# SSD chunks of a hybrid encoder step: decay multiply and D term of the chunks taken off GpSimd

## The chip, the cores and the metric

The kernel runs on one core of one Trainium2 chip. The metric is the device time of one execution in microseconds, the median of several executions. The core's engines are named PE (TensorE, matrix products), DVE (VectorE), ACT (ScalarE), POOL (GpSimd) and SP (which issues DMAs). Each runs its own instructions in a fixed order and waits for the others by semaphores.

## The reference, cut to what matters

One layer of an encoder is run on 592 columns: 16 meta tokens, 512 prompt tokens, 64 sample tokens. Three branches share one input projection: a Mamba-2 SSD branch, an S5 branch with a gated linear unit (GLU), and stick-breaking attention. Each is lifted to 1024 channels, weighted by a sigmoid gate and summed; an output projection and an MLP follow. The change is in the SSD branch:

```python
    decay = jnp.exp(jnp.where(causal, seg, -jnp.inf))
    cb = jnp.einsum('bcign,bcjgn->bcijg', cm, bm)
    y_diag = jnp.einsum('bcijgh,bcjghp->bcighp', cb[..., None] * decay * dt[:, :, None], x)
    to_end = jnp.exp(a_cum[:, :, -1:] - a_cum) * dt
    blk_states = jnp.einsum('bcjgn,bcjgh,bcjghp->bcghpn', bm, to_end, x)
    ...
    y_off = jnp.einsum('bcign,bcghpn,bcigh->bcighp', cm, s_in, jnp.exp(a_cum))
    ...
    y = y[:, front:front + T] + d_skip.reshape(SSD_GROUPS, SSD_HPG)[:, :, None] * xs
    y = y.reshape(bsz, T, SSD_WIDTH) * jax.nn.silu(z)
```

There are 16 heads of 64 channels. `x` times `to_end` feeds the state of the next chunk; `d_skip` times `x`, one number per head, is added to the output.

## The kernel before

**Dense work.** Every projection is split into tiles of 288 output columns. Operands are split into a high and a low part, so each 128-deep step k is three matmuls (L336, L337, L338, in `mm3`). A tile of the GLU and of the attention lift has four steps (12 matmuls), the others eight (24). The result `ps_d` lies in one of three PSUM buffers (pool `psd`), and the next tile in that buffer waits until ACT or DVE has read it. The GLU runs for m in 0..7: two sigmoid tiles, which ACT reads (`gls`, L250) before DVE multiplies `gt` by it, then two product tiles, which DVE reads as `mix<-ps_d,gt`. The attention lift (`ocx`) follows, then the SSD lift `la`, which reads `yah` and `yal` for k = 0..7. Weights are split by ACT (`w_hi`, L253) and DVE (`w_lo`, L217).

**Side work.** The SSD branch is a generator, `ssd`, from which the dense loop pulls steps while GLU and lift run. It goes over six chunks: chunk 0 of 16 columns, chunks 1 to 4 of 128, chunk 5 of 64. For each chunk `turned` transposes on PE (`ps_bt`, `ps_x`), copies `bt` on ACT (L1240) and multiplies x by dt on DVE (`xd`). `late_x` multiplies `xd` by `tend` into `xe` (L1260). `decay` has ACT take Exp of half of `ar` into `a` twice (L1270), DVE subtract 16 times (L1272), ACT take Exp of `ar` (L1273). `weigh` multiplies `ar` by `cb` on DVE and sets `ya` to x times D (L1285). `outputs` multiplies on PE into `ps_y` (L1318), `state` into `ps_st` (L1293), and `gather` adds `ps_y` to `ya` on DVE. After the last chunk `ya` is gated, normed and split into `yah` (ACT, L257) and `yal` (DVE), which `la` reads.

**Order.** The instructions of all engines are put in order by a scheduler that simulates a timeline of the whole program; the source gives dependences, priorities (`urgent` for weights and for reading `ps_d`) and the order within a pulled step. An edit of one step can thus move instructions far from it. Sigmoid and Exp need different ACT tables, and going from one to the other is an `ACT_TABLE_LOAD`.

Of the kernel before, what the change touches and what calls it, by code (L numbers as in the profile page):

```python
# [11 lines left out]
AF = mybir.ActivationFunctionType  # L12
OP = mybir.AluOpType
# [163 lines left out]
def body(tc, io):  # L177
    nc = tc.nc
    V, S, G, PE, SP = nc.vector, nc.scalar, nc.gpsimd, nc.tensor, nc.sync
# [4 lines left out]
    with ExitStack() as ctx:  # L184
# [13 lines left out]
        A = lambda n, i=0, w=1: pa[:, PA[n][0] + i:PA[n][0] + i + w]  # L198
# [17 lines left out]
        def tt(e, o, a, b, op):  # L216
            e.tensor_tensor(o, a, b, op=op)  # L217
# [226 lines left out]
        with urgent():  # L444
            for ps, cols in zip(pss, halves):
                n = cols.stop - cols.start
# [757 lines left out]
        def ssd():  # L1204
            yp = late["y"] = tc.alloc_tile_pool(name="late_y", bufs=1)
            ya = late["ya"] = yp.tile([128, 8, T], F32, name="ya", tag="x2")
            dp = tc.alloc_tile_pool(name="ssd", bufs=1)
            d2 = tc.alloc_tile_pool(name="ssd2", bufs=2)
            dt, acm, tend, bd = (sv[n] for n in ("dt", "acm", "tend", "bd"))
# [46 lines left out]
            def late_x(c):  # L1256
                t0, n = chunks[c]
                e = env[c]
                e["xe"] = xe = dp.tile([128, 16, 64], F32, name="xe", tag="xe")
                tt(G, xe[:n], e["xd"][:n], tend[:n, c, :].unsqueeze(2).to_broadcast([n, 16, 64]), OP.mult)  # L1260

            def decay(c):

# [14 lines left out]
            def weigh(c):  # L1278
                t0, n = chunks[c]
                e = env[c]  # L1280
                ar, cb = e["ar"], e["cb"]
                for g in range(2):
                    tt(V, ar[:n, 8 * g:8 * g + 8, :n], ar[:n, 8 * g:8 * g + 8, :n],
                       cb[:n, g, :n].unsqueeze(1).to_broadcast([n, 8, n]), OP.mult)
                tt(G, ya[:, :, t0:t0 + n], e["xc"][:, 0:8, :n], A("d_ssd", 0, 8).unsqueeze(2).to_broadcast([128, 8, n]),  # L1285
                   OP.mult)

            def state(c, st):
                t0, n = chunks[c]
# [41 lines left out]
            yield  # L1331
            turned(0)
            late_x(0)
            yield
            st = state(0, None)
            turned(1)
            late_x(1)
            fetch_chunk(2)
            yield
# [25 lines left out]
            for c in range(1, 6):  # L1365
                if c < 5:
                    turned(c + 1)
                weigh(c)
                if c == 5:
                    normed(0, 0)  # L1370
# [19 lines left out]
                if c < 5:  # L1390
                    late_x(c + 1)
# [80 lines left out]
        for m2 in range(4):  # L1472
            w = None
            for j in range(2):
                m = 2 * m2 + j
# [186 lines left out]
```

## Time and profile before

| | |
|---|---|
| median of three runs | 1111.87 us (1111.23, 1111.87, 1114.11) |
| the profiled execution | 1113.19 us, span 1111.5 us, granted clock 0.998 |
| PE busy | 1095.5 us |
| DVE busy | 795.7 us |
| ACT busy | 540.7 us |
| POOL busy | 125.4 us |

The span is the profiled stretch of one execution; the 1.7 us to its time are start and end around it. Times are microseconds; a granted clock of 1.00 is TensorE's full 2.4 GHz. In a timeline a row is a run of like instructions: start, length, engine, line, operation, output and inputs, shape, count, and in brackets idle time before it with what released it. Matmuls are pipelined: one takes 0.29 us and the next starts 0.13 us after it.

### The profile page before, as it was taken

What the parts mean: (1) busy time and instruction counts of PE and PEld (TensorE: products, weight loads), DVE (VectorE), ACT (ScalarE), POOL (GpSimd) and SP (SyncE); (2) the same over time, 40 slices, a digit from 0 to 9 for tenths busy, and PEclk for the clock granted to TensorE, in tenths of its full rate; (3) what the DMA queues carried; (4) which work ended last, traced back from release to release, by engine and by line L of the source; (5) the groups of instructions that cost most, each with busy time, mean ns of one, the idle gap of its engine ahead of it and who ended that gap; (6) DMA issues with size and microseconds to landing.
All of it is one profiled execution on the core that took longest, in us unless ns stands there. A gap on an engine that the chain in (4) does not pass through costs nothing.

```text
span 1111.5 us, 21286 instructions
## 1 busy us (share of the span) xinstructions
PE 1095.5 (99%) x8532; PEld 1056.3 (95%) x8532; DVE 795.7 (72%) x1390; ACT 540.7 (49%) x928; POOL 125.4 (11%) x193
## 2 busy tenths in 40 slices
PE   9999999999999999999999999999999999999998
PEld 8998999999998999897888999999999999999998
DVE  7968579965767466468989754477867776786787
ACT  6465466633365545365657333354444444444443
POOL 1087233011000000021310001200000000000000
PEclk9999999999999999999999999999999999999999
DMA  7653223566754353187445533222232223123222
GB/s 274 149 138 114 94 80 132 136 190 171 222 178 151 112 169 136 64 267 247 133 139 178 173 109 115 99 76 77 76 114 80 74 84 123 60 77 133 77 82 80
DMA packets 80594, 144.04 MB, mean 130 GB/s; under 512 B 26512, under 2 KB 40688, under 8 KB 79984
## 3 DMA queue, kind: packets, MB, share of 16 engines
q1 hardware_dynamic: 80496, 142.69, 41.7%
q8 instruction: 67, 1.10, 0.4%
q14 instruction: 31, 0.25, 0.1%
HBM read 117.40 MB, written 24.38 MB: 128 GB/s over the span
## 4 chain that ended last, share of the span: by engine, by line
PE 83%; DVE 8%; ACT 3%; POOL 2%; issue 2%; DMA 2%; SPq 1%; POOLq 0%; ACTq 0%; DVEq 0%
PE ps_d L336 19%; PE ps_d L337 19%; PE ps_d L338 18%; PE ps_x L1581 3%; PE ps_x L1580 3%; PE ps_x L1582 3%; PE ps_o L895 2%; PE ps_z L895 2%; PE ps_y L1581 1%; PE ps_y L1580 1%; PE ps_y L1582 1%; PE ps_y L1318 1%; DVE w_lo L217 1%; DVE ya L217 1%; PE ps_z L1581 1%
## 5 line engine op out<-in xcount | busy, mean ns | idle before, releaser
L253 ACT ACTIVATE w_hi<-w_raw 128x1024 fp32r<-128x1024 f32 (+1 forms) x150 | 151.9, 1012 | 219.8 <-PE ps_d L337 142.2
L336 PE MATMUL ps_d<-hh,w_hi 128*128 128x288 f32 (+1 forms) x864 | 258.2, 299 | 0.0
L337 PE MATMUL ps_d<-hl,w_hi 128*128 128x288 f32 (+1 forms) x864 | 258.0, 299 | 0.0
L338 PE MATMUL ps_d<-hh,w_lo 128*128 128x288 f32 (+1 forms) x864 | 258.0, 299 | 0.0
L217 DVE TENSOR_TENSOR w_lo<-w_raw,w_hi 128x1024 fp32r<-128x1024 f32 (+1 forms) x150 | 180.3, 1202 | 95.2 <-ACT w_hi L253 91.9
L337 PEld LDWEIGHTS ps_d<-hl,w_hi 128*128 128x128 f32 x864 | 162.6, 188 | 0.9 <-issue 0.3
L338 PEld LDWEIGHTS ps_d<-hh,w_lo 128*128 128x128 f32 x864 | 162.6, 188 | 0.6
L336 PEld LDWEIGHTS ps_d<-hh,w_hi 128*128 128x128 f32 x864 | 162.7, 188 | 0.2
L336 PE MATMUL ps_d<-x2h,w_hi 128*128 128x288 f32 x512 | 151.2, 296 | 0.0
L337 PE MATMUL ps_d<-x2l,w_hi 128*128 128x288 f32 x512 | 151.1, 295 | 0.0
L338 PE MATMUL ps_d<-x2h,w_lo 128*128 128x288 f32 x512 | 150.3, 295 | 0.0
L336 PEld LDWEIGHTS ps_d<-x2h,w_hi 128*128 128x128 f32 x512 | 96.2, 188 | 0.1
L338 PEld LDWEIGHTS ps_d<-x2h,w_lo 128*128 128x128 f32 x512 | 96.2, 188 | 0.1
L337 PEld LDWEIGHTS ps_d<-x2l,w_hi 128*128 128x128 f32 x512 | 96.2, 188 | 0.0
L253 ACT ACTIVATE w_hi<-ws 128x1024 fp32r<-128x1024 f32 x32 | 34.0, 1061 | 55.0 <-PE ps_y L1581 21.6
L1581 PE MATMUL ps_x<-ftl,w_hi 128*128 128x288 f32 x192 | 56.7, 295 | 0.5 <-DVE ftl L217 0.5
L1580 PE MATMUL ps_x<-fth,w_hi 128*128 128x288 f32 x192 | 56.8, 296 | 0.2 <-ACT s L1600 0.2
L1582 PE MATMUL ps_x<-fth,w_lo 128*128 128x288 f32 x192 | 56.4, 294 | 0.0
L1531 ACT ACTIVATE fr<-ps_d 128x288 f32<-128x288 f32 x64 | 25.7, 402 | 55.8 <-PE ps_d L338 55.8
L217 DVE TENSOR_TENSOR w_lo<-ws,w_hi 128x1024 fp32r<-128x1024 f32 x32 | 39.1, 1220 | 12.6 <-ACT w_hi L253 12.6
L336 PE MATMUL ps_d<-ybx,w_hi 128*128 128x288 f32 x128 | 39.7, 310 | 3.0 <-DVE mix L217 2.3
L906 DVE TENSOR_TENSOR_SCAN aw<-col,aw 128x400 f32<-128x400 f32 (+4 forms) x36 | 30.7, 898 | 16.6 <-ACT aw L250 16.6
(471 smaller groups left out, 2643.3 us busy)
## 6 DMA issues: line engine op xcount, KB each, us to landing
w_raw<-wts SPq DMA_DIRECT2D x150, 512.0 KB, 3.5
g_scr<-go SPq DMA_DIRECT2D x24, 288.0 KB, 2.8
gt<-g_scr SPq DMA_DIRECT2D x24, 288.0 KB, 3.0
ar<-ac_scr SPq DMA_DIRECT2D x4, 1024.0 KB, 7.5
x_scr<-cs SPq DMA_DIRECT2D x10, 297.5 KB, 3.1
xc<-x_scr SPq DMA_DIRECT2D x4, 640.0 KB, 7.4
xt<-xT SPq DMA_DIRECT2D x8, 296.0 KB, 5.6
z_scr<-zs SPq DMA_DIRECT2D x8, 288.0 KB, 5.0
```

Source lines behind the costliest of these rows:

```text
L217: e.tensor_tensor(o, a, b, op=op)
L253: S.activation(hi, x, AF.Copy)
L336: PE.matmul(ps, wh[:, c], xh[:, k, cols], start=start and k == 0, stop=False)
L337: PE.matmul(ps, wh[:, c], xl[:, k, cols], start=False, stop=False)
L338: PE.matmul(ps, wl[:, c], xh[:, k, cols], start=False, stop=stop and k == kt - 1)
L895: mm = lambda *a, **b: PE.matmul(*a, skip_group_check=True, **b)
L906: V.tensor_tensor_scan(x, one.to_broadcast([128, n]), x, 1.0, op0=OP.mult, op1=OP.mult)
L1318: PE.matmul(py[oo, 128 * (h // 2):128 * (h // 2) + n], a, b, start=step == 0, stop=step == 1, skip_group_check=True)
L1531: S.activation(r[:, cols], ps, AF.Relu)
L1580: PE.matmul(ps, w[0][:, o], fh[:, k], start=first and k == 0, stop=False, skip_group_check=True)
L1581: PE.matmul(ps, w[0][:, o], fl[:, k], start=False, stop=False, skip_group_check=True)
L1582: PE.matmul(ps, w[1][:, o], fh[:, k], start=False, stop=k == 3, skip_group_check=True)
```

## The change

In `late_x` the product of `xd` and `tend`, six times in a run, goes from POOL to DVE. In `weigh` the product of x and D of a chunk, one POOL instruction for eight blocks of 128 channels, becomes eight ACT copies, one for each block, with D as a scale that differs by partition: 40 copies for chunks 1 to 5, of 128 columns (32) or 64 (8). POOL keeps two memsets there.

```diff
             def late_x(c):
...
-                tt(G, xe[:n], e["xd"][:n], tend[:n, c, :].unsqueeze(2).to_broadcast([n, 16, 64]), OP.mult)
+                tt(V, xe[:n], e["xd"][:n], tend[:n, c, :].unsqueeze(2).to_broadcast([n, 16, 64]), OP.mult)
...
             def weigh(c):
...
-                tt(G, ya[:, :, t0:t0 + n], e["xc"][:, 0:8, :n], A("d_ssd", 0, 8).unsqueeze(2).to_broadcast([128, 8, n]),
-                   OP.mult)
+                for m in range(8):
+                    S.activation(ya[:, m, t0:t0 + n], e["xc"][:, m, :n], AF.Copy, scale=A("d_ssd", m))
```

The scheduler puts all engines in another order. On ACT, from the `bt` of chunk 4 on, before:

```order
L1240 ACTIVATE bt<-ps_bt 128x128
L253 ACTIVATE w_hi<-w_raw 128x1024
L1270 ACTIVATE a_6029<-ar 64x1024 x2
L250 ACT_TABLE_LOAD
L250 ACTIVATE gls<-ps_d 128x288 x2
L253 ACTIVATE w_hi<-w_raw 128x1024
L250 ACTIVATE gls<-ps_d 128x288
L1273 ACT_TABLE_LOAD
L1273 ACTIVATE ar<-ar 128x2048
L1240 ACTIVATE bt<-ps_bt 64x128
L250 ACT_TABLE_LOAD
L250 ACTIVATE gls<-ps_d 128x288
```

and now, from the `bt` of the same chunk on (`ya<-xc,pa` are the new copies, of chunk 3 and, 64 wide, of chunk 5):

```order
L1240 ACTIVATE bt<-ps_bt 128x128
L1286 ACTIVATE ya<-xc,pa 128x128 x8
L250 ACT_TABLE_LOAD
L250 ACTIVATE gls<-ps_d 128x288
L1270 ACT_TABLE_LOAD
L1270 ACTIVATE a_6050<-ar 64x1024 x2
L253 ACTIVATE w_hi<-w_raw 128x1024
L1286 ACTIVATE ya<-xc,pa 128x64 x8
L250 ACT_TABLE_LOAD
L250 ACTIVATE gls<-ps_d 128x288
L1273 ACT_TABLE_LOAD
L1273 ACTIVATE ar<-ar 128x2048
```

The next two are a table load and the third sigmoid. Between the first sigmoid and the third stood nothing but one `w_hi`; now four table loads, both Exps and eight copies stand there, and eight copies ahead of the first. Over the whole program the table loads go from 33 to 34.

On DVE, a little ahead of that, from the end of chunk 2 into chunk 3, before:

```order
L217 TENSOR_TENSOR ya<-ps_y,ya 128x8x128
L217 TENSOR_TENSOR mix<-ps_d,gt 128x288
L217 TENSOR_TENSOR st<-st,ps_st 128x512
L217 TENSOR_TENSOR cb<-ps_bt,cst 128x128 x2
L217 TENSOR_TENSOR mix<-ps_d,gt 128x288
L217 TENSOR_TENSOR w_lo<-w_raw,w_hi 128x1024
L1272 TENSOR_SCALAR ar<-ar,acm 128x128 x8
```

and now, at the same place:

```order
L217 TENSOR_TENSOR st<-st,ps_st 128x512
L217 TENSOR_TENSOR xe<-xd,tend 128x1024
L217 TENSOR_TENSOR ya<-ps_y,ya 128x8x128
L217 TENSOR_TENSOR cb<-ps_bt,cst 128x128 x2
L217 TENSOR_TENSOR gt<-gt,gls 128x288
L217 TENSOR_TENSOR xd<-ps_x,dt 128x512
L217 TENSOR_TENSOR mix<-ps_d,gt 128x288
L1272 TENSOR_SCALAR ar<-ar,acm 128x128 x16
```

The `xe` is new on DVE, ahead of `gather`; and where the two `mix` of a GLU unit stood with three short instructions between them, the second one now comes after the 16 subtractions (and after `a`, `st`, `xd` and `ar` times `cb`, which follow).

On PE the `ps_y` of chunks 1 to 5 stand 7, 17, 36, 36 and 53 matmuls later in the dense stream than before, and the first `la` tiles are woven. Before, two tiles followed each other (the number is the PSUM tile's):

```order
L336 MATMUL ps_d_7716<-yah_6567,w_hi_7572 128x288
L337 MATMUL ps_d_7716<-yal_6568,w_hi_7572 128x288
L338 MATMUL ps_d_7716<-yah_6567,w_lo_7573 128x288
L336 MATMUL ps_d_7742<-yah_6567,w_hi_7572 128x288
L337 MATMUL ps_d_7742<-yal_6568,w_hi_7572 128x288
L338 MATMUL ps_d_7742<-yah_6567,w_lo_7573 128x288
```

and now three tiles first do k = 0 to 3 each, and then take turns:

```order
L337 MATMUL ps_d_7814<-yal_6603,w_hi_7675 128x288
L338 MATMUL ps_d_7814<-yah_6602,w_lo_7676 128x288
L336 MATMUL ps_d_7751<-yah_6602,w_hi_7607 128x288
L336 MATMUL ps_d_7777<-yah_6602,w_hi_7607 128x288
L336 MATMUL ps_d_7814<-yah_6602,w_hi_7675 128x288
L337 MATMUL ps_d_7751<-yal_6603,w_hi_7607 128x288
```

The first two rows are the end of the third tile's k = 3; behind them the steps k = 4 to 7 of all three tiles stand.

## Rows read from the trace of the kernel before

**Rows 1.** Page, busy time, share and instructions of each engine.
```profile
PE 1095.5 (99%) x8532; PEld 1056.3 (95%) x8532; DVE 795.7 (72%) x1390; ACT 540.7 (49%) x928; POOL 125.4 (11%) x193
```

**Rows 2.** Busy time by stretch: PE, PEld, DVE, ACT, POOL, then granted clock.
```profile
540.00:560.00 20.00, 18.12 (x152) 15.84 (x149) 18.45 (x42) 12.59 (x15) 5.79 (x4) 0.91 0.32 92
...
554.00:556.00 2.00, 2.00 (x10) 2.00 (x10) 2.00 (x4) 1.52 (x3) 0.00 (x0) 0.51 0.24 69
556.00:558.00 2.00, 2.00 (x12) 2.00 (x11) 2.00 (x4) 0.41 (x1) 0.00 (x0) 0.64 0.04 8
```

**Rows 3.** PE's waits from 480 to 660 us: total us, times, longest.
```profile
PE ps_d L336 <- DVE mix L217: 2.3, 3, 1.9
...
PE ps_d L336 <- ACT gls L250: 0.6, 1, 0.6
```

**Rows 4.** POOL, 480 to 620 us, by form: busy, mean ns, idle before.
```profile
L217 POOL TENSOR_TENSOR ya<-xc,pa 128x1024 f32<-128x1024 f32 x4 | 8.6, 2149 | 0.1
L217 POOL TENSOR_TENSOR xe<-xd,tend 128x1024 f32<-128x1024 f32 x4 | 7.6, 1906 | 46.5 <-PE ps_st L1293 36.0 <-DVE xd L217 10.5
```

**Rows 5.** Timeline of DVE: start, length, instructions.
```profile
484.36 3.94 DVE L1272 TENSOR_SCALAR ar<-ar,acm 128x128 f32<-128x128 f32 x16 [1.20 <-ACT a L1270]
488.23 1.21 DVE L217 TENSOR_TENSOR a<-a,xc 128x1024 f32<-128x1024 f32 x1
...
521.05 3.22 DVE L1272 TENSOR_SCALAR ar<-ar,acm 128x128 f32<-128x128 f32 x16
...
565.85 1.66 DVE L217 TENSOR_TENSOR ya<-ya,zl 128x288 f32<-128x288 f32 x1
...
568.65 0.45 DVE L217 TENSOR_TENSOR ya<-ya,zl 128x288 f32<-128x288 f32 x1
```

**Rows 6.** Timeline of POOL beside the fourth of them.
```profile
565.29 1.90 POOL L217 TENSOR_TENSOR xe<-xd,tend 64x1024 f32<-64x1024 f32 x1 [14.87 <-PE ps_st L1293]
```

**Rows 7.** ACT copies by form, 480 to 622 us, and one run of them.
```profile
L257 ACT ACTIVATE yah<-ya,sg 128x576 fp32r<-128x576 f32 x8 | 5.7, 766 | 6.3 <-DVE ya L217 6.3
...
L1240 ACT ACTIVATE bt<-ps_bt 128x128 f32<-128x128 f32 x4 | 1.1, 276 | 3.5 <-PE ps_bt L1238 3.5
...
603.17 2.10 ACT L257 ACTIVATE yah<-ya,sg 128x576 fp32r<-128x576 f32 x3
```

**Rows 8.** Timeline of ACT behind the `bt` of chunk 4.
```profile
531.64 2.14 ACT L1270 ACTIVATE a<-ar 64x1024 f32<-64x1024 f32 x2 [0.78 <-DMA ar<-ac_scr]
533.80 1.28 ACT L250 ACT_TABLE_LOAD   x1
535.10 0.71 ACT L250 ACTIVATE gls<-ps_d 128x288 f32<-128x288 f32 x2
537.33 1.06 ACT L253 ACTIVATE w_hi<-w_raw 128x1024 fp32r<-128x1024 f32 x1 [1.52 <-PE ps_d L337]
539.05 0.41 ACT L250 ACTIVATE gls<-ps_d 128x288 f32<-128x288 f32 x1 [0.66 <-PE ps_d L338]
...
541.33 1.91 ACT L1273 ACTIVATE ar<-ar 128x2048 f32<-128x2048 f32 x1
```

**Rows 9.** Timeline of PE there: chunk matmuls, dense matmuls, transposes.
```profile
538.95 0.71 PE L1318 MATMUL ps_y<-ar,xd 128*64 128x128 f32 x8
...
544.37 0.40 PE L336 MATMUL ps_d<-ybx,w_hi 128*128 128x288 f32 x1
...
544.87 0.30 PE L336 MATMUL ps_d<-ybx,w_hi 128*128 128x288 f32 x1
545.00 0.30 PE L337 MATMUL ps_d<-ybx,w_hi 128*128 128x288 f32 x1
...
548.98 1.03 PE L1252 MATMUL ps_x<-cst,xc 128*64 128x128 f32 x8
```

**Rows 10.** Timelines: the last `yal` on DVE, the first `la` matmul on PE.
```profile
619.81 0.81 DVE L258 SCALAR_TENSOR_TENSOR yal<-ya,sg,yah 128x576 fp32r<-128x576 f32 x1
...
620.10 0.38 PE L336 MATMUL ps_d<-yah,w_hi 128*128 128x288 f32 x1 [0.19 <-issue]
```

## The prediction

> **What bounds the kernel now.** I read the page's busy row first: PE is busy 1095.5 of 1111.5 us [rows 1]. The kernel is bound by TensorE, and nothing in the change adds or removes a matmul. So the change costs what it makes PE wait, and gains what it takes off PE's waits; busy time on the other engines counts only where PE waits for it. POOL with 125.4 us and ACT with 540.7 have room on average, DVE with 795.7 less [rows 1]. An average says little, so I read the stretch in which the SSD chunks run. Between 540 and 560 us PE is busy 18.12 of 20 at a mean granted clock of 0.91 [rows 2], and the table of PE's waits says why: from 480 to 660 us it waits 2.3 us for `mix` on DVE, 1.9 of it at once, and 0.6 us for a sigmoid on ACT [rows 3]. Behind the long wait the clock drops to near its lower level of 1.2 GHz: 10 and then 12 matmuls start in 2 us each, at 0.51 and 0.64 [rows 2], where a start every 0.133 us [rows 9] gives 15. These eight fewer cost 8 x 0.133 = 1.1 us. I call this place 2; what it could give back is 1.9 + 1.1 = 3.0 us. That is the whole credit the change can find in the stretch, beside some tenths.
>
> **What the change takes off POOL.** Four `xe` of 1.9 us and four `ya` of 2.1 us [rows 4] and their smaller kin go. Nothing shows PE waiting for them: no POOL line is among PE's waits [rows 3], and POOL itself idled 46.5 us before its four `xe` [rows 4]. For the path this is worth nothing by itself. One thing does come off DVE: an instruction that runs beside a POOL one takes longer. The 16 subtractions take 3.94 us beside an `xe` and 3.22 otherwise, and a 288-column product takes 1.66 instead of 0.45 [rows 5], ending at 567.51, just after the `xe` that runs from 565.29 to 567.19 [rows 6]. There are five such stretches, of which these are the first and the last; their excesses are 0.7 to 1.2 us and sum to about 5.0.
>
> **What it adds on DVE.** An `xe` on DVE is a product of two 128x1024 operands in SBUF, as `a<-a,xc` is, which takes 1.21 us [rows 5]. Six make at most 7.3 us, against 5.0 returned: net +2 on an engine with 28% idle [rows 1]. Each stands ahead of `gather` and delays that by 1.2 us. `ps_y` is next written more than ten dense tiles later, so this is hidden by dense work; if that cover were gone it would cost 1.2 us a chunk. I take 0.
>
> **What it adds on ACT.** No row shows a copy scaled by partition of 128 columns. The nearest is `bt`, an unscaled copy of 128 columns at 0.276 us; `yah` is a scaled one of 576 columns at 0.766 [rows 7]. From `bt` to `w_hi` with 1024 columns at 1.06 [rows 8] a column costs (1.06 - 0.276)/896 = 0.875 ns, so an unscaled 576 would be 0.67, and the scale costs 0.10. In a run, three `yah` take 2.10 and not 3 x 0.766 = 2.30 [rows 7], so each of a run saves 0.10. One copy lies then between 0.18 (0.276 less the overlap, scale free) and 0.37 (scale paid, no overlap). I take 0.27, with both: eight are 2.2 us, eight of 64 columns (0.056 less each) 1.7, all forty 10.3. ACT goes to about 551 us and is still half idle, so the sum of ACT does not matter; where the copies stand does.
>
> The Trainium skill ("ScalarE: Activation LUTs", What ACT_TABLE_LOAD costs) gives a copy with one per-partition operand 186 + 93 + 0.833 ns a column, less 93 in a run, an estimate of 2.4 us for eight of 128 columns; my sum by it would be 0.3 us longer. The same page (Rules for kernel authors) has multiplications on VectorE and not on ScalarE, which speaks against this half of the change; no run here shows that yet.
>
> **Place 1, the term that decides.** It lies behind the `bt` of chunk 4, where the two orders of ACT are set side by side in the section on the change. Before, the Exp, load and sigmoids there took ACT from 531.64 on [rows 8], and PE met no wait: no other tile waits for a sigmoid longer than 0.6 us [rows 3]. The second Exp (1.91 us at 541.33 [rows 8]) with its two loads ran while PE worked on 5.4 us of chunk matmuls, `ps_y`, `ps_st` and transposes, from 538.95 to 544.37 [rows 9], which need no `ps_d` buffer. In the new order the `ps_y` of chunk 3 comes only behind seven dense tiles, so PE goes through dense tiles alone, and ACT has more to do before it reads them. I count both from the `bt` of chunk 4.
>
> ACT: `bt` 0.28, eight copies 2.2, load 1.28, sigmoid 0.41, load 1.28, two Exps 2.14, `w_hi` 1.06, eight small copies 1.7, load 1.28, sigmoid 0.41 [rows 7, 8]. That is 12.0 us until the second sigmoid there, the first tile of the next GLU unit, is read; 0.2 less with the overlaps of neighbours, 11.8. PE: 12 starts of 0.133 make a tile of 1.6 us [rows 9], five tiles are 8.0, and two `ps_x` groups add 0.45 each (half of the 0.8 to 1.0 us of the double group at 548.98 [rows 9]), 8.9 in all. Then the three buffers hold two unread sigmoid tiles and a product tile whose `mix` stands on DVE behind the 16 subtractions and what follows them. The sixth tile waits until 11.8: **2.9 us**. The seventh waits for the third sigmoid, behind a load, the Exp of `ar`, a load and itself: 1.28 + 1.91 + 1.28 + 0.41 = 4.9, less the 1.6 of the sixth tile: **3.3 us**. Place 1 costs 6.2 us. With copies at 0.18 it is 4.7, at 0.37 it is 7.7. Both are waits over 1.9 us, so a fall of the clock as at place 2 can come on top; its price there was 1.1.
>
> **Place 2 and the rest.** The second products of chunk 4 still stand behind the subtractions of chunk 5, with copies and loads ahead on ACT. I leave its 3.0 us where they are: 0, between -3.0 and +0.5. At the end of the SSD branch everything is later by the 53 matmuls that the last `ps_y` moved, 53 x 0.133 = 7.0 us. `yal` for the last k is written by 620.62 and would have been needed at 620.10 + 21 x 0.133 = 622.9 [rows 10], a slack of 2.3. The remaining 4.7 meet the woven first tiles: three times 12 matmuls, 4.8 us, can run before any k = 4. If all run ahead it costs 0; if only one tile does, 4.7 - 1.6 = 3.1. The order is made for the first, so I take 0.5.
>
> The sum is 6.2 + 0 + 0 + 0.5 = +6.7 us. The profiled execution took 1113.19, so the same one would take 1119.9; it lies 1.3 above the median of 1111.87, on which the forecast stands: 1118.6.
>
> **The rivals.** *The two shifts cancel.* Copies cost 0.18, so that place 1 is 4.7, and place 2 vanishes since the buffers come free in another order: +4.7 - 3.0 + 0 = +1.7, 1113.6. For it: ACT is idle half the time, and the waits of before hang on a few instructions [rows 3]. Against it: most of what place 1 waits for is table loads and Exps, whose prices are in the rows. *Faster.* POOL no longer holds DVE up, DVE gets its 5.0 us back just where PE waited for it, and place 2 goes with its clock (-3.0) and the sigmoid wait of 0.6 too: 1108.3. This decides if ACT is through with its queue at place 1 by the 8.9 us of the five tiles, 2.9 us sooner than I count; the four loads and Exps there would have to start before the tiles do. For it speaks the DVE row at 565.85 [rows 5, 6].
>
> The Trainium skill ("SBUF — State Buffer", Who interferes with whom) has this as an exclusive lock of a port pair that DVE and GpSimd share; the trace agrees, with 1.66 us for 0.45.
>
> *Heavier.* Place 1 at its upper price (+1.5), a half-clock stretch behind it (+1.1), and the tail at 3.1 (+2.6): +11.9, 1123.8.
>
> **How the numbers follow.** A measurement here can tell about 0.3%, 3.3 us: below 1108.5 is faster, above 1115.2 slower. My forecast, +3.3 to +10, has 0.48; heavier 0.15; the two shifts cancel, within 0.3%, 0.27; faster 0.10. So faster 0.10, same 0.27, slower 0.63. The range leaves out the faster case and the end of the heavy one: 1110.0 to 1125.0, from a cancelled place 1 with a little gain to the heavy case and one microsecond.
>
> **What would show it.** Right: PE waits behind the `bt` of chunk 4 for sigmoids (L250) of about 3 us twice, with a granted clock below 1 after them; the eight copies take 2.2 us in the ACT timeline and an `xe` on DVE 1.2; no DVE instruction is stretched as at 565.85; POOL's busy time falls by at least the 16.2 us of its eight large ones [rows 4] with no wait of PE changed by it. Wrong: copies as long as 0.37, or PE's longest waits still for `mix` alone; no wait for a sigmoid over 1 us would fell place 1. A wait of the first `la` tiles for `yah` or `yal` above 1 us would show the tail mis-sized.

## The result, and the profile after

| | before | after |
|---|---|---|
| median | 1112.99 us (1111.23 to 1114.53) | 1126.09 us (1125.11 to 1129.05) |
| profiled execution | 1113.19 us, span 1111.5 | 1125.11 us, span 1123.3 |

The ratio is 1.0113, with a 95% interval from 1.0088 to 1.0137: the change costs 12.6 us. I had forecast +6.7 us, with the range ending at 1125.0. The direction was right, the size about half, and the time lies above the range.

The busy row of the page of the kernel after answers to [rows 1]:

```profile
PE 1098.3 (98%) x8532; PEld 1057.4 (94%) x8532; DVE 796.5 (71%) x1396; ACT 553.0 (49%) x969; POOL 103.8 (9%) x182
```

POOL gives up 21.6 us, ACT takes on 12.3, DVE only 0.8, and the span grows by 11.8. None of these sums explains that. PE does: its idle time goes from 16.0 us (1111.5 - 1095.5) to 25.0, and its busy time, for the same matmuls, grows by 2.8. Total waits of PE from 480 to 660 us (total us, times, longest), to be held against [rows 3]:

```profile
PE ps_d L336 <- ACT gls L250: 7.9, 4, 3.6
PE ps_d L336 <- DVE mix L217: 2.1, 2, 1.1
```

Waits for sigmoids go from 0.6 to 7.9 us, and the lift `la` now waits for `yah` and `yal` (rows below). By stretch (PE, PEld, DVE, ACT, POOL, then granted clock), there are now two stretches with a clock below 1, where [rows 2] had one:

```profile
540.00:560.00 20.00, 14.74 (x131) 11.61 (x130) 14.29 (x27) 13.66 (x27) 0.95 (x1) 0.91 0.39 108
560.00:580.00 20.00, 17.08 (x147) 14.01 (x145) 15.19 (x36) 10.69 (x14) 0.96 (x1) 0.91 0.25 66
```

**Place 1.** The timeline of ACT behind the `bt` of chunk 4, in the kernel after (start, length, instructions):

```profile
531.77 0.28 ACT L1240 ACTIVATE bt<-ps_bt 128x128 f32<-128x128 f32 x1 [1.65 <-PE ps_bt L1238]
531.94 2.44 ACT L1286 ACTIVATE ya<-xc,pa 128x128 f32<-128x128 f32 x8
534.40 1.28 ACT L250 ACT_TABLE_LOAD   x1
...
540.55 2.00 ACT L1286 ACTIVATE ya<-xc,pa 128x64 f32<-128x64 f32 x8
542.57 1.28 ACT L250 ACT_TABLE_LOAD   x1
543.86 0.41 ACT L250 ACTIVATE gls<-ps_d 128x288 f32<-128x288 f32 x1
544.29 1.28 ACT L1273 ACT_TABLE_LOAD   x1
545.58 1.91 ACT L1273 ACTIVATE ar<-ar 128x2048 f32<-128x2048 f32 x1
547.51 1.28 ACT L250 ACT_TABLE_LOAD   x1
```

ACT is busy without a gap from 531.77 on, and reads the second sigmoid tile at 543.86. PE, in its own timeline, stands before the sixth tile until then:

```profile
544.32 0.61 PE L336 MATMUL ps_d<-ybx,w_hi 128*128 128x288 f32 x1 [3.56 <-ACT gls L250]
...
545.21 0.44 PE L336 MATMUL ps_d<-ybx,w_hi 128*128 128x288 f32 x1
...
549.27 0.40 PE L336 MATMUL ps_d<-ybx,w_hi 128*128 128x288 f32 x1 [1.70 <-ACT gls L250]
...
551.04 0.66 PE L1318 MATMUL ps_y<-ar,xd 128*64 128x128 f32 x8
```

With the end of the first wait the clock falls (the granted clock is 0.57 from 544 to 548 us) and the tile runs at a start every 0.24 us, so that it takes 2.9 us in place of 1.6; that eats part of the second wait. Behind the second wait the granted clock is 1.00. The chunk matmuls `ps_y`, which need no `ps_d` buffer, begin at 551.04, when both waits are over.

**Place 2** and the end of the branch, in PE's timeline:

```profile
566.73 0.40 PE L336 MATMUL ps_d<-ybx,w_hi 128*128 128x288 f32 x1 [1.08 <-DVE mix L217]
570.43 0.40 PE L336 MATMUL ps_d<-ybx,w_hi 128*128 128x288 f32 x1 [1.84 <-ACT gls L250]
...
634.75 0.66 PE L336 MATMUL ps_d<-yah,w_hi 128*128 128x288 f32 x3 [0.95 <-ACT yah L257]
635.77 0.40 PE L337 MATMUL ps_d<-yal,w_hi 128*128 128x288 f32 x1 [0.36 <-DVE yal L258]
```

Where the loss is collected can be read from the first matmul of a stage. The first of the attention lift (`ocx`), and the first of the output projection (`mxh`), which ends the mixing, in the kernel before:

```profile
591.13 0.29 PE L336 MATMUL ps_d<-ocx,w_hi 128*128 128x288 f32 x1
...
671.21 0.29 PE L336 MATMUL ps_d<-mxh,w_hi 128*128 128x288 f32 x1
```

and after:

```profile
598.79 0.30 PE L336 MATMUL ps_d<-ocx,w_hi 128*128 128x288 f32 x1
...
682.01 0.29 PE L336 MATMUL ps_d<-mxh,w_hi 128*128 128x288 f32 x1
```

The lag is 7.7 us at the end of the GLU, 10.8 at the end of the lifts, and 11.8 at the end of the run. It is still 10.8 at the last matmul (1106.63 and 1117.42) and at the issue of the last output transfer (1108.31 and 1119.10): the last 1.0 us lies behind all of PE's work.

### The profile page after: what moved, and what is told of

The parts are those of the page before. It is cut to its first block, busy times and chain, and to the rows that moved or that the text cites. A ratio compares the mean times of both kernels' runs of the same rounds, so it can differ in the third digit from the quotient of the medians.

```text
span 1123.3 us, 21309 instructions
## 1 busy us (share of the span) xinstructions
PE 1098.3 (98%) x8532; PEld 1057.4 (94%) x8532; DVE 796.5 (71%) x1396; ACT 553.0 (49%) x969; POOL 103.8 (9%) x182
## 4 chain that ended last, share of the span: by engine, by line
PE 80%; DVE 8%; ACT 5%; DMA 3%; issue 2%; POOL 2%; SPq 1%; ACTq 0%; DVEq 0%; POOLq 0%
PE ps_d L336 18%; PE ps_d L337 18%; PE ps_d L338 18%; PE ps_x L1581 3%; PE ps_x L1580 3%; PE ps_x L1582 3%; PE ps_o L895 2%; PE ps_z L895 2%; PE ps_y L1581 1%; PE ps_y L1580 1%; PE ps_y L1582 1%; PE ps_y L1318 1%; DVE w_lo L217 1%; DMA xc<-x_scr 1%; PE ps_z L1581 1%
## 5 line engine op out<-in xcount | busy, mean ns | idle before, releaser
L217 DVE TENSOR_TENSOR w_lo<-w_raw,w_hi 128x1024 fp32r<-128x1024 f32 (+1 forms) x150 | 177.4, 1183 | 103.4 <-ACT w_hi L253 102.8
L253 ACT ACTIVATE w_hi<-ws 128x1024 fp32r<-128x1024 f32 x32 | 34.0, 1062 | 55.3 <-PE ps_y L1581 21.6
L217 DVE TENSOR_TENSOR w_lo<-ws,w_hi 128x1024 fp32r<-128x1024 f32 x32 | 39.0, 1220 | 12.7 <-ACT w_hi L253 12.6
```

The lines of the kernel that those rows point to most:

```text
L253: S.activation(hi, x, AF.Copy)
```

## The experiments

Two kinds of theory stood after the result. A: what costs is ACT's queue between the reads of two sigmoid tiles, and in it the table loads. B, C and D put the loss into the moved work: into the SSD branch as a whole, the DVE side and its order, or the copies. Ratios are against the kernel before, run beside each.

**The loads taken out, the order kept.** Sigmoid is (1 + tanh(x/2))/2, and in the kernel as built tanh needs no table load between it and Exp. But for the loads, every engine goes through its instructions in the same order as without the edit, and the products on DVE that take up the 1 and the 1/2 last 0.45 us as before.

```diff
-                sigmoid(ps, s[:, cols])
-                tt(V, g[:, cols], g[:, cols], s[:, cols], OP.mult)
+                S.activation(s[:, cols], ps, AF.Tanh, scale=0.5)
+                V.scalar_tensor_tensor(g[:, cols], s[:, cols], 1.0, g[:, cols], op0=OP.add, op1=OP.mult)
...
-                tt(V, mix[:, m, cols], ps, g[:, cols], OP.mult)
+                V.scalar_tensor_tensor(mix[:, m, cols], ps, 0.5, g[:, cols], op0=OP.mult, op1=OP.mult)
```

In the changed kernel:

> The changed kernel with the GLU's sigmoid written as (1 + tanh(x/2))/2: tanh lies in the same ACT table as Exp, so 12 table loads go (34 to 22) and the order of all engines stays. Theory A (the loss is ACT's queue between the reads of sigmoid tiles, loads included): at place 1 ACT has 1.28 us less ahead of the first read, 3 loads (3.85) less ahead of the second, 5 (6.4) less ahead of the third, so the waits of 3.56 and 1.70 us and the half clock between them go (6.7 us), and the 1.84 us at place 2 with its half clock (3.3): about 1126 - 10 = 1116 us. Theory B (the moved work itself, 40 ACT copies and 6 xe on DVE, holds up the SSD branch): this work is all still there, and the time stays within 3 us of 1126. Theory C (the new order of DVE and PE is bad, whatever ACT does): 1123 to 1126, the waits turn into waits for mix.

Measured: 1113.29 us, ratio 0.9993 (0.9979 to 1.0007). In sum the whole loss is gone, 2.7 us more than I expected. ACT's timeline at place 1:

```profile
531.38 2.44 ACT L1286 ACTIVATE ya<-xc,pa 128x128 f32<-128x128 f32 x8
533.73 0.39 ACT L1462 ACTIVATE gls<-ps_d 128x288 f32<-128x288 f32 x1
...
537.51 2.02 ACT L1286 ACTIVATE ya<-xc,pa 128x64 f32<-128x64 f32 x8
539.44 0.39 ACT L1462 ACTIVATE gls<-ps_d 128x288 f32<-128x288 f32 x1
539.73 1.90 ACT L1273 ACTIVATE ar<-ar 128x2048 f32<-128x2048 f32 x1
541.54 0.39 ACT L1462 ACTIVATE gls<-ps_d 128x288 f32<-128x288 f32 x1
```

All 40 copies are still there, at the same length, and all `xe` are on DVE; the second sigmoid is read at 539.44 and the third at 541.54. PE's waits for `gls` from 480 to 660 us fall to one of 0.2 us, while those for `yah` stay:

```profile
PE ps_d L336 <- ACT yah L257: 0.9, 1, 0.9
...
PE ps_d L336 <- ACT gls L1462: 0.2, 1, 0.2
```

The same two marks as above show where the time came back:

```profile
587.53 0.30 PE L336 MATMUL ps_d<-ocx,w_hi 128*128 128x288 f32 x1
...
670.17 0.29 PE L336 MATMUL ps_d<-mxh,w_hi 128*128 128x288 f32 x1
```

The GLU ends 11.3 us sooner than in the changed kernel, and even 3.6 sooner than in the kernel before: here no half clock falls at place 2, and PE idles 2.2 us between 480 us and the first `ocx` against 3.2. The lifts take 82.6 us, against 83.2 in the changed kernel and 80.1 before: that part of the loss is still there. So the loads made the loss in the GLU, and the sum comes out at nothing because a gain in the GLU meets a loss in the lifts; that the two are equal is luck. Theories B, C and D fall as causes of the loss in the GLU. In the kernel before:

> The kernel before with the same rewriting of the sigmoid: the loads fall from 33 to 22, the order stays. Theory A: before, PE waits only 0.6 us for a sigmoid, and its long wait (1.88 us, and the half clock behind it) is for a product on DVE, so taking the loads away gives at most 1 us: 1111.5 to 1113. If loads cost PE time wherever they stand (rival), 11 loads of 1.28 us would give back several us here too, as many as in the changed kernel: about 1103.

Measured: 1113.25 us, ratio 0.9993 (0.9981 to 1.0005). Eleven loads less are worth nothing there, as A has it. A load costs here only where PE waits behind it.

**The same work in another order.** One number was altered, in both kernels: the pace at which the dense loop pulls steps of the branch.

```diff
-PACE = {"s5_parts": 1.25, "s5": 1.35, "attention": 1.8, "ssd": 1.1}
+PACE = {"s5_parts": 1.25, "s5": 1.35, "attention": 1.8, "ssd": 1.0}
```

> The changed kernel with one number altered, the pace at which steps of the SSD branch are pulled (1.1 to 1.0): the same instructions in another order. On ACT the two sigmoids of a unit now stand side by side (gls x2) where the changed kernel has a table load, the Exp of ar and a load between them; 32 loads in place of 34. Theory A: the 1.70 us wait goes and most of the 3.56 with it: 1113 to 1117 us. Theory B (moved work costs): 1124 to 1128, since the work is the same.

Measured: 1112.35 us, ratio 0.9990 (0.9974 to 1.0007). The time is as theory A has it, but only in part for the reason that I gave. The second and the third sigmoid now stand side by side, and the wait of 1.70 us is gone. The wait of 3.56 is gone as well, though ACT's queue behind the `bt` of chunk 4 is the same up to the second sigmoid, to 0.1 us:

```profile
542.62 1.28 ACT L250 ACT_TABLE_LOAD   x1
543.91 0.71 ACT L250 ACTIVATE gls<-ps_d 128x288 f32<-128x288 f32 x2
```

What differs is DVE and PE. In the changed kernel DVE reads the second product tile ahead of this sigmoid only behind the 16 subtractions:

```profile
546.25 0.45 DVE L217 TENSOR_TENSOR mix<-ps_d,gt 128x288 f32<-128x288 f32 x1
```

so that no buffer is free for the sixth tile until ACT reads one. Now it reads both product tiles ahead of the subtractions:

```profile
537.15 0.81 DVE L217 TENSOR_TENSOR mix<-ps_d,gt 128x288 f32<-128x288 f32 x2
```

PE goes through the sixth tile without a wait, and then has the matmuls of chunk 3 from 542.19 to 547.6:

```profile
542.19 0.44 PE L1318 MATMUL ps_y<-ar,xd 128*64 128x128 f32 x4
...
546.53 1.08 PE L1293 MATMUL ps_st<-xe,bt 128*64 128x512 f32 x4
```

In the changed kernel they begin at 551.04, behind seven dense tiles where there are six here. So a buffer that is free sooner, and one tile in PE's order, let PE work while ACT goes through its queue, loads and all. The order differs in other places too, and none of these differences was tested by itself. The lifts take 84.0 us (first `ocx` at 585.92, first `mxh` at 669.90): the loss there stays in this order as well. For the kernel before:

> The kernel before with the same pace of 1.0: what a redrawn order alone does to a kernel without the change. Theory A: orders differ by the waits that they happen to make, one or two of 1 to 3 us and a half-clock stretch of 1.7: within +-4 us of 1112. If the kernel before stood in an unusually good order that any edit destroys (rival), this one loses as much as the change did, about 1124.

Measured: 1115.16 us, ratio 1.0015 (1.0001 to 1.0028). The program has 36 loads, as many as any other here, and loses 0.3% at most. The number of loads does not tell the time, and this redraw shows no sign that the kernel before stood in a rare good order.

**Each half alone.**

```diff
-                tt(G, xe[:n], e["xd"][:n], tend[:n, c, :].unsqueeze(2).to_broadcast([n, 16, 64]), OP.mult)
+                tt(V, xe[:n], e["xd"][:n], tend[:n, c, :].unsqueeze(2).to_broadcast([n, 16, 64]), OP.mult)
```

> Only the first half of the change: xe on DVE, the D term still one POOL instruction a chunk. The order has at place 1 what the changed kernel has without the copies: a load, both Exps and two more loads between the sigmoids (36 loads in all). If the loads and Exps between the sigmoids are the cause (theory A), it loses without any copy: the queue there is 4.4 us shorter (2.4 + 2.0 of copies), which takes the 3.56 us wait away; the wait for the third sigmoid is then 2 to 3 us, with a half clock behind it of 1.4 and place 2 as in the changed kernel (+1): 1116 to 1120. If the copies are the cause (theory D), 1112 to 1114.

Measured: 1121.66 us, ratio 1.0065 (1.0042 to 1.0087), 1.7 us over the expected end. Without a single copy more than half of the loss is there. PE's order is nearly that of the changed kernel (18 of 8532 matmuls elsewhere, against 182 between this run and the kernel before), so it is this half that moved the chunk matmuls. PE's waits:

```profile
PE ps_d L336 <- ACT gls L250: 5.2, 3, 2.9
PE ps_d L336 <- DVE mix L217: 2.8, 2, 1.8
```

The other half:

```diff
-                tt(G, ya[:, :, t0:t0 + n], e["xc"][:, 0:8, :n], A("d_ssd", 0, 8).unsqueeze(2).to_broadcast([128, 8, n]),
-                   OP.mult)
+                for m in range(8):
+                    S.activation(ya[:, m, t0:t0 + n], e["xc"][:, m, :n], AF.Copy, scale=A("d_ssd", m))
```

> Only the second half: D times x as 40 ACT copies, xe still on POOL. ACT's order has 33 loads; at place 1 the sigmoids of a unit stand side by side (gls x2) with the copies ahead of or behind them and no load between. Theory A: the copies alone cost what PE then waits for one read, 0 to 4 us, with at most one half-clock stretch: 1112 to 1117. Theory D (the copies are the cause): 1120 to 1126.

Measured: 1119.70 us, ratio 1.0049 (1.0034 to 1.0063), above A's range and below D's. PE's waits:

```profile
PE ps_d L336 <- DVE mix L217: 4.8, 2, 3.9
PE ps_d L336 <- ACT gls L250: 4.0, 3, 2.4
```

So neither half alone makes the whole loss; each draws an order in which PE waits. Whether that again hangs on the loads was tested on both, with the edit of the tanh above:

> Only the first half (xe on DVE), with the sigmoid as tanh: same order as with the sigmoid, 22 loads in place of 36. Theory A: the 5.2 us of waits for sigmoids and the half clock behind the longest go, the waits for mix shrink to what DVE itself causes: the loss of +7 us falls to 0 to +2, about 1113 to 1116. If xe on DVE is a load of its own on the path (theory C), the loss stays over +4.

Measured: 1114.42 us, ratio 1.0008 (0.9991 to 1.0025). The waits for sigmoids are gone; one of 2.9 us for `mix` is left, with a granted clock of 1.00 behind it, and it costs no measurable time in sum.

> Only the second half (D times x as ACT copies), with the sigmoid as tanh, 22 loads in place of 33. With the sigmoid its largest wait was 3.9 us for mix on DVE, whose own inputs come from ACT. Theory A: that wait and the 4.0 us for sigmoids both go back to the loads, and the time is that of before, -1.5 to +1.5: 1111.5 to 1115. Theory D (copies are the cause): the wait for mix stays, and +4 or more.

Measured: 1111.65 us, ratio 0.9977 (0.9962 to 0.9993). The 3.9 us wait for `mix` went with the loads too; that it did so by way of the DVE instructions that wait for ACT ahead of it is inferred:

```profile
PE ps_d L336 <- DVE mix L1466: 1.7, 2, 0.9
...
PE ps_d L336 <- ACT gls L1462: 1.0, 1, 1.0
```

This is the one version whose interval lies wholly below the kernel before, by 0.23%, which is less than the 0.3% that I count as told apart: D on ACT, `xe` still on POOL, tanh for the sigmoid.

**Both products on DVE, none on ACT.**

```diff
-                for m in range(8):
-                    S.activation(ya[:, m, t0:t0 + n], e["xc"][:, m, :n], AF.Copy, scale=A("d_ssd", m))
+                tt(V, ya[:, :, t0:t0 + n], e["xc"][:, 0:8, :n], A("d_ssd", 0, 8).unsqueeze(2).to_broadcast([128, 8, n]),
+                   OP.mult)
```

> Both products on DVE, nothing on ACT or POOL: xe and, as one instruction of 1.2 us a chunk, D times x; 33 loads. Measures the change with no copy on ACT. Theory A: time goes by where the loads fall between sigmoids, 1112 to 1120. If DVE were the bound (theory C), twelve products of 1.2 us more than in the kernel before would show as waits for mix and gt, longer than the 2.1 us of mix in the changed kernel, and 1122 or more.

Measured: 1121.36 us, ratio 1.0061 (1.0040 to 1.0082), 1.4 us above A's end. PE waits again for ACT first, though ACT has no new work, then 2.9 us for `gt`, and 2.8 us for `yah` at the first `la` tile:

```profile
PE ps_d L336 <- ACT gls L250: 4.5, 3, 2.3
...
PE ps_d L336 <- ACT yah L257: 2.8, 1, 2.8
```

The loss here was not taken apart further; the loads were not taken out of this order, so for it the cause is read from the waits alone.

**Shorter copies in the order of the change.** The copies carry a constant scale, so the D term is another.

```diff
-                    S.activation(ya[:, m, t0:t0 + n], e["xc"][:, m, :n], AF.Copy, scale=A("d_ssd", m))
+                    S.activation(ya[:, m, t0:t0 + n], e["xc"][:, m, :n], AF.Copy, scale=2.0)
```

> The changed kernel with the copies scaled by a constant 2.0 in place of the column D (so this part of the output is another), which shortens each copy and leaves the order up to place 2 as it is: it prices the scale by column. A copy that falls from 0.30 us in a run to 0.20 makes eight 1.6 in place of 2.45. Theory A: the queue at place 1 is 16 x 0.1 = 1.6 us shorter, and the wait of 3.56 becomes about 2.0; the second stays 1.70 or grows by a little: total 1123.5 to 1125. If ACT's queue were not what PE waits for, the wait of 3.56 stays.

Measured: 1120.03 us (1118.95 to 1123.80), ratio 1.0050 (1.0031 to 1.0069): by the ratios 7 us less than the change, more than A's 1 to 2.6. The copies became shorter as expected, in ACT's timeline:

```profile
534.54 1.70 ACT L1286 ACTIVATE ya<-xc 128x128 f32<-128x128 f32 x8
...
542.41 1.26 ACT L1286 ACTIVATE ya<-xc 128x64 f32<-128x64 f32 x8
```

and PE's waits at place 1 fell from 3.56 and 1.70 to 0.54 and 1.51, without a half clock there, while a wait of 1.27 for `mix` stands ahead of them:

```profile
543.05 0.40 PE L336 MATMUL ps_d<-ybx,w_hi 128*128 128x288 f32 x1 [1.27 <-DVE mix L217]
...
545.45 0.40 PE L336 MATMUL ps_d<-ybx,w_hi 128*128 128x288 f32 x1 [0.54 <-ACT gls L250]
...
550.41 0.40 PE L336 MATMUL ps_d<-ybx,w_hi 128*128 128x288 f32 x1 [1.51 <-ACT gls L250]
```

So 1.5 us off the queue took 3.2 us off the two waits and the half clock behind them, and a third wait took 1.3 back. This trace is of the slowest of the runs (1123.8). In it PE still waits 7.3 us for `gls` from 480 to 660 us, 3.1 of them at once at place 2, where the order differs; so the sum is not settled. That PE waits for ACT's queue at place 1 is.

**An attempt at more.** With tanh, the copies moved from `weigh` into `gather`, ahead of the addition there:

```diff
             def weigh(c):
...
-                for m in range(8):
-                    S.activation(ya[:, m, t0:t0 + n], e["xc"][:, m, :n], AF.Copy, scale=A("d_ssd", m))
...
             def gather(c):
...
                 o = ya[:, :, t0:t0 + n]
+                for m in range(8):
+                    S.activation(ya[:, m, t0:t0 + n], e["xc"][:, m, :n], AF.Copy, scale=A("d_ssd", m))
```

> The changed kernel with the sigmoid as tanh, and the copies of a chunk issued one step later in the SSD branch, just ahead of the addition of ps_y (in gather). Theory A: with the loads gone the copies are the longest thing between reads of sigmoids, and where they stand matters by at most their 2.45 us: 1109 to 1114, no worse than the changed kernel with tanh alone.

Measured: 1114.86 us, ratio 1.0010 (0.9993 to 1.0027), 0.9 above the expected range: nothing won. With the pace at 1.15:

> The same with the branch pulled at pace 1.15 in place of 1.1, so that yah and yal for the first la tiles are due a little sooner: an attempt at a kernel faster than both. Waits of 0.5 to 0.6 us for DVE products, no half-clock stretch, and one wait of up to 3 us for yah ahead of la: 1106 to 1111. If the order is a draw without a direction, 1111 to 1117.

Measured: 1117.78 us, ratio 1.0029 (1.0012 to 1.0047). It lies above both ranges, and the expected gain did not come. PE's largest waits are now one for `yah`, where the branch hands over to `la`, and one ahead of the GLU:

```profile
PE ps_d L336 <- ACT yah L257: 3.5, 1, 3.5
PE ps_d L336 <- ACT go L250: 2.2, 1, 2.2
```

`go` is the gate's sigmoid ahead of the GLU, which still needs the sigmoid's table: two Exps, eight copies and a load of 1.28 us stand before it on ACT.

## Why the prediction was right in direction and half in size

**Place 1 was the right place, and nearly the right price.** I had waits of 2.9 and 3.3 us for two sigmoids, 6.2 in sum; they measured 3.56 and 1.70, and the half clock between them 12 x 0.24 - 1.6 = 1.3, so 6.6. Copies took 2.44 and 2.00 us in place of 2.2 and 1.7, which is most of what the first wait has over. The Trainium skill's figure ("ScalarE: Activation LUTs", What ACT_TABLE_LOAD costs), an estimate of 2.4 us for eight, was the better one; for both groups of copies it would have made my sum 0.5 us longer, and not 0.3. The second wait is smaller since the tile ahead of it ran at half clock. [rows 2] showed a half clock behind a wait of 1.9 us, and yet I put it into a rival and not into the sum.

**The end of the branch was the step that failed most.** I took 0.5, between 0 and 3.1, since the woven order was made for the case in which all three first tiles run ahead. It measured 3.1: the way from the first `ocx` to the first `mxh` grew from 80.1 to 83.2 us. The first `la` tiles wait 0.20 + 0.95 + 0.36 = 1.5 us against 0.2 before, and the `ocx` tiles 0.4 more than before. Of the rest, 1.4, some 0.5 is a pair of matmuls `ps_n` that stood ahead of this stretch before, and most of what is left lies beside the waits: around the wait of 0.95, 1.24 us pass from one start to the next and 0.24 to the one after, where two steps of 0.13 would do; that is 0.27 more than the wait itself, and PE stops seven times in this stretch where it stopped four times.

The runs show with which half this loss goes. With `xe` on DVE the lifts take 82.6 to 84.0 us, with table loads or without (the changed kernel, with tanh, at pace 1.0, with plain copies, with late copies; `xe` alone, with and without tanh). With `xe` on POOL they take 79.1 to 80.4 (the kernel before, with tanh, at pace 1.0; D alone, with and without tanh). Two kernels more have matmuls of chunk 5 inside the lifts and do not compare. The last `yal` ends 38.5 to 40.3 us behind the first `ocx` in the former, 29.2 to 30.5 in the latter. I had priced this half at 0 on the path. Whether the 1.2 us of each `xe` or the order that they draw makes the branch so late is not shown.

**Place 2 failed too.** I left it at 0, with an upper bound of +0.5. It measured 1.08 + 1.84 of waits, 2.9 in place of the 1.9 of before, and a second half clock as before: about +1.0. I had seen that copies and loads stand ahead of the sigmoids there too, and did not count ACT's queue there as I had at place 1.

These three make 6.6 + 1.0 + 3.1 = 10.7 of the 10.8 us that PE is late. The last 1.0 us, from the last output transfer to the end of the span (4.2 us in place of 3.2), does not go with the change: the changed kernel with tanh has 4.2 as well and loses nothing, at pace 1.0 it has 3.2. What makes it stays open.

**What held.** The `xe` on DVE took 1.22 us each, against the 1.21 taken from [rows 5]. POOL no longer stretches DVE: the gating products average 0.45 us, and not one is as long as the 1.66 of [rows 5]. DVE from 480 to 620 us, by form:

```profile
L217 DVE TENSOR_TENSOR ya<-ya,zl 128x288 f32<-128x288 f32 x16 | 6.8, 448 | 0.0
L217 DVE TENSOR_TENSOR xe<-xd,tend 128x1024 f32<-128x1024 f32 x4 | 4.9, 1216 | 0.0
```

DVE's busy time rose by 0.8 us where I had 2. The sum did not matter, as forecast.

**The rivals.** Faster and the cancelled shifts did not come; the point that decided for them, that ACT is through by the 8.9 us of five tiles, lay 3.6 us off. The heavier case was the nearest. Its +11.9 is what the two profiled executions differ by, but that is luck in part: its half clock (1.1) and its tail (3.1) came, its dearer place 1 did not (waits of 5.3 us, not 7.7), and place 2 and the end of the span, which it left at 0, made up for that. Its 1123.8 stood on a median of 1111.87, and the median of before came to be 1112.99; 1125.0 as the end of the range left one microsecond for all of this.

**What I had not seen.** I took the order as given and asked what it costs. The runs showed that this was the smaller question. Where the loads are out, the 40 copies on ACT and the six products on DVE cost nothing in sum. What costs in the GLU is loads of 1.28 us between reads of sigmoid tiles, in an order that leaves PE neither a free buffer nor chunk matmuls while ACT goes through them. Taking out the loads gives back 11.3 us ahead of the lifts; the order at pace 1.0, which still has 32 loads, gives back 12.9. Of what the change costs in the lifts, 3.1 us, the one gives back 0.6 and the other nothing.

## What to carry to other kernels

When an edit redraws the order of all engines, price the places where the engine that bounds the time waits on a queue, and look there for table loads: what counts is not how many there are but whether the bounding engine has other work and a free buffer meanwhile. Where two functions of different tables alternate on ACT, writing one by a function of the other's table can make the kernel depend less on the order: the ratios of six kernels with tanh lie between 0.9977 and 1.0029, those of the seven with the sigmoid between 0.9990 and 1.0113. The Trainium skill ("ScalarE: Activation LUTs", Rules for kernel authors) says to do all of one table set before switching; these runs agree where PE waited behind the loads (12 loads and 12.6 us in the changed kernel), and show no gain where it did not (11 loads in the kernel before). Behind a long wait, allow for a half clock in the sum: it followed the waits of 3.56 and 1.84 us here, but not one of 2.93 (`xe` alone, with tanh) nor one of 2.65 (the kernel before at pace 1.0), where the granted clock stayed at 1.00. Read the loss by stages before calling a sum of nothing free, and run one redrawn order of the same work before blaming the work.

## What the runs showed of the hardware that I had not expected

Tanh and Exp alternated without a load between them, at 0.39 us for a tile of 288 columns, against 0.41 for the sigmoid. A load is 1.28 us, and the next instruction starts 0.01 to 0.02 us behind it (load at 534.40, sigmoid at 535.69 in the kernel after): nothing more is seen of a switch. A scale that differs by partition costs 0.09 us on each short copy: eight of 128 columns took 2.44 us with it and 1.70 with a constant.
